# A two-layer decoder trunk: Norm's rows one product later in the convolution and the first MLP product, every second low part of the next operand behind the weights' low part

## The chip, the cores and the metric

The kernel runs on one core of one Trainium2 chip. The metric is the device time of one execution in microseconds (us), lower is better. TensorE (PE) has a queue of its own for weight loads (PEld); VectorE (DVE), ScalarE (ACT), GpSimd (POOL) and SyncE (SP, which issues most transfers) each work through their instructions in the order in which they were written down for that engine.

## The reference

Two residual layers over 1024 tokens of width 1024, all in fp32; layer 0 has an attention and pooling mixer, layer 1 a short gated convolution. Each layer then has cross-attention into 256 memory tokens and a squared-ReLU MLP of width 4096. Every sub-layer begins with an RMS norm.

```python
def rms_norm(x, g):
    xf = x.astype(jnp.float32)
    y = xf * lax.rsqrt(jnp.mean(xf * xf, axis=-1, keepdims=True) + EPS)
    return (y * g.astype(jnp.float32)).astype(x.dtype)
...
def odd_mixer(h, w_in, conv_w, w_out):
    S = h.shape[1]
    proj = h @ w_in
    b_gate = proj[..., :CONV_DIM]
    c_gate = proj[..., CONV_DIM:2 * CONV_DIM]
    z = c_gate * proj[..., 2 * CONV_DIM:]
    zp = jnp.pad(z, ((0, 0), (CONV_WIDTH - 1, 0), (0, 0)))
    y = zp[:, 0:S] * conv_w[0]
    for tap in range(1, CONV_WIDTH):
        y = y + zp[:, tap:tap + S] * conv_w[tap]
    return (b_gate * y) @ w_out
...
def sq_relu_mlp(h, w1, w2):
    a = jax.nn.relu(h @ w1)
    return (a * a) @ w2
...
    for l in range(DEPTH):
        ...
        h = h + cross_attention(rms_norm(h, norm_xattn_g[l]), mem_n,
                                xattn_wq[l], xattn_wkv[l], xattn_wo[l])
        h = h + sq_relu_mlp(rms_norm(h, norm_mlp_g[l]), mlp_w1[l], mlp_w2[l])
    return rms_norm(h, final_norm_g)
```

## The kernel before, in words

Activations lie transposed in SBUF: eight tiles of 128 channels x 1024 tokens. A matrix product keeps fp32 accuracy with three matmuls in place of one: operand and weight are each cut into a high part (a rounded copy, made by ACT: `h` tiles, `wh`) and a low part (the rest, made by DVE: `l` tiles, `wl`), and high x high, low x high and high x low are added up in PSUM. The cut is two instructions, L72 and L73:

```python
            nc.scalar.activation(hi, src, AF.Copy)
            nc.vector.tensor_sub(lo, src, f32(hi))
```

**Products.** The convolution's input projection, the query projection and both MLP matrices run as `split_steps`: a 2x2 block product in seven steps (i = 0 to 6) of 12 matmuls 128x512 each, with sums of operand blocks and of weight blocks in place of the eighth step. The operand has four groups of four tiles (`m0A0_g_j` is group g, tile j of chunk 0 of the MLP's hidden operand in layer 0; `m0x_g_j` is the convolution's operand, `c0o_x_g_j` that of layer 0's first MLP matrix). The weights are cut into four groups as well, `wh81_0`/`wl81_0` to `wh81_3`/`wl81_3` for weight pair 81; steps 0 and 1 use group 0, steps 2 and 3 group 1, and so on. `w_next()` runs at steps 0, 2, 4 and 6 and writes down the cut of a group one ahead of its use, so group 0 of the next product is cut at step 6. Of `wh` and `wl` there are two buffers each. A first-group cut also writes the sums of the weight halves (L162, L163, L165, L166: 128x512 on DVE). After a step `out(i)` moves a PSUM bank to SBUF (ACT copy or DVE add, at high priority).

**Hooks.** All other work (the next sub-layer's cuts, squares, taps, loads and stores) is hung on the steps as `hooks`: `{step: [functions]}`. At step i the weight cut is written down first, then the hooks, then the twelve matmuls and `out(i)`. A tile scheduler makes the final order of each engine from this, and each engine then keeps to it.

**Norm.** The row norms aren't applied to the operand; the product runs on the raw operand and its result is scaled by a row vector. `Norm.stage1` transposes the sum of squares on PE (eight 128x128 transposes, L354), reduces it on DVE (L355, L357) and takes the power -1/2 on POOL (L358, `rcol`). `Norm.stage2` spreads `rcol` over the partitions with eight PE transposes (L367) and copies them with ACT (L369, `rbc`).

**Layer stages by name.** `m0a`p / `m1a`p: product p (0 to 15) of the first MLP matrix in layer 0 / 1; `m0b`c`_`p: the second matrix, chunk c (0 to 3), product p (0 to 3); `cv`j`c`, `cv`j`x`, `cv`j`b`: the three projections of the convolution for channel pair j (0 to 3); products 0 and 1 of `ma`, and c and x of cv0, run in turns. `mlp.up` writes the first matrix's products, `prepare` the cuts of the next chunk's operand (`fetch` loads, `ready` cuts). The gate, the taps and the scaling of the convolution for pair j are hooks of its `b` product. The conv product's squares of `rbc` (`squared`) feed the gate.

Of the kernel before, what the change touches and what calls it, by code (L numbers as in the profile page):

```python
# [40 lines left out]
def hybrid_trunk(ctx: ExitStack, tc: tile.TileContext, xT, memT, vecs, lams, rel, onehot, negrow, invcnt,  # L41
# [284 lines left out]
    def merged(*hooks):  # L326
        return {i: [f for h in hooks for f in h.get(i, ())] for i in range(7)}
# [70 lines left out]
    X = Act()  # L398
# [513 lines left out]
    X, nrm = residual(Y, G_X[0], "X1", split=True)  # L912
# [140 lines left out]
    def mlp(l, X, nrm, g_next, name):  # L1053
# [46 lines left out]
        def fetch(c, g, js=range(KT // 2)):  # L1100
            def run():
                for j in js:
                    t = slot(f"{name}f{c}_{g}_{j}")
                    raw[c, g, j] = t if g < 3 else t[:, :H]
                    nc.sync.dma_start(raw[c, g, j], gd[4 * c + j][g])

            return run

        def ready(c, g, js=range(KT // 2)):
            def run():  # L1110
                for j in js:
                    A[c].group(g, j, raw.pop((c, g, j)))

            return run


        def prepare(c, left):
            if left == 3:
                return {1: [fetch(c, 0, (0, 1))], 4: [ready(c, 0, (0,))], 5: [ready(c, 0, (1,))]}
            if left == 2:  # L1120
                return {1: [fetch(c, 0, (2, 3))], 4: [ready(c, 0, (2,))], 5: [ready(c, 0, (3,))]}
            if left == 1:
                return {2: [fetch(c, 1)], 4: [fetch(c, 2)], 5: [ready(c, 1, (0,))], 6: [ready(c, 1, (1, 2)), fetch(c, 3)]}
            if left == 0 and c == 0:
                return {0: [ready(c, 1, (3,))], 2: [ready(c, 2, (1,))], 3: [ready(c, 2, (2,))], 4: [ready(c, 3, (2, 3))]}
            return {0: [ready(c, 1, (3,))], 1: [ready(c, 2, (0,))], 2: [ready(c, 2, (1, 2))],
                    3: [ready(c, 2, (3,))], 4: [ready(c, 3)]} if left == 0 else {}

        rest, ahead = merged(X.late, {5: [nrm.stage1], 6: [nrm.stage2]}), []
        r0, one = up(0, rest, False)  # L1130
        rest, two = up(1, {4: r0[1], 5: r0[2], 6: r0[3]}, False)
        in_turns(one, two)
        rest = merged(rest, {4: r0[5]})
        for p in range(2, 2 * KT):
            if p == 2 * KT - 1:
                ahead.extend(h_load(i, f"{name}b0") for i in range(2))
# [3 lines left out]
        rest = {}  # L1140
# [16 lines left out]
        def first_group(p):  # L1157
            nx.group(0, p, raws_x[p, 0])
# [6 lines left out]
        def get(g):  # L1165
            for p in range(2):
                x = slot(f"{name}xf{g}_{p}")
                raws_x[p, g] = x if g < 3 else x[:, :H]
                nc.sync.dma_start(raws_x[p, g], xd[p, g])

        def made(g, *ps):
            for p in ps:
                nx.group(g, p, raws_x.pop((p, g)))
        for c in range(4):
            for p in range(KT // 2):
                t, ahead = ahead, []
# [23 lines left out]
                if c == 0 and p < 2:  # L1200
                    todo.append(late[p])
                if tail and not fin:
                    todo.append({2: [lambda: get(1)], 4: [lambda: made(1, 0)],
                                 5: [lambda: scale(t, p, 0), lambda: first_group(p), lambda: made(1, 1)],
                                 6: [lambda: made(1, 2), lambda: get(2)]})
                elif tail:
                    todo.append({3: [squares_of(0, 0)], 5: [squares_of(1, 0)], 6: [squares_of(1, 1), lambda: nn.stage1((0,))]})
                steps = split_steps(A[c], f"{name}b{c}_{p}", evac, merged(*todo), tail=tail)
# [49 lines left out]
    def conv_mixer(X, nrm, g_next, name):  # L1258
        Y, ys = Halves(), {}
        sq = {}  # L1260

        def product(nm, hooks, first=False, run=True):
            r = [slot(f"{nm}_r{n}") for n in range(2)]

            def evac(n, h, ps, new):
                d = r[n][:, half(h)]
                if new:
                    nc.scalar.activation(d, ps, AF.Copy)
                else:
                    nc.vector.tensor_add(d, d, ps)  # L1270

            steps = split_steps(X, nm, evac, hooks, first=first)
            if not run:
                return r, steps
            for _ in steps:
                pass
            return r

        def parts(k):
            return lambda: Y.put(f"{name}g{k}_", k, ys.pop(k))  # L1280

        def squared():
            sq[0] = slot(f"{name}_rsq")
            nc.scalar.activation(sq[0], nrm.rbc, AF.Square)

        for j in range(KT // 2):
            nm, last = f"{name}{j}", j == KT // 2 - 1
            if j == 0:
                c, one = product(f"{nm}c", X.late[0], first=True, run=False)
                x, two = product(f"{nm}x", X.late[1], run=False)  # L1290
                in_turns(one, two)
            else:
                c = product(f"{nm}c", merged(before, {4: [parts(0)]} if last else {}))
                x = product(f"{nm}x", {1: [parts(1)], 3: [parts(2)]} if last else {})

            def gate(n, c=c, x=x):
                def run():
                    nc.vector.tensor_mul(c[n], c[n], x[n])
                    nc.vector.tensor_mul(c[n], c[n], sq[0])
                return run  # L1300

            def taps(n, z=c, j=j):
                def run():
                    k = 2 * j + n
                    y = ys[k] = slot(f"{name}_y{k}")
                    nc.scalar.activation(y, z[n], AF.Copy, scale=col(C_CONV + 16 + k))
                    for d in (1, 2):
                        nc.vector.scalar_tensor_tensor(y[:, d:], z[n][:, : S - d], col(C_CONV + 8 * (2 - d) + k),
                                                       y[:, d:], op0=ALU.mult, op1=ALU.add)
                return run  # L1310

            def scaled(n, j=j):
                return lambda: nc.vector.tensor_mul(ys[2 * j + n], ys[2 * j + n], nrm.rbc)

            hooks = {0: [gate(0)], 1: [taps(0)], 2: [gate(1)], 3: [taps(1)], 4: [scaled(0)], 5: [scaled(1)]}
            if j == 0:
                hooks = {1: [nrm.stage2, squared], 2: [gate(0)], 3: [taps(0)], 4: [gate(1)], 5: [taps(1)],
                         6: [scaled(0), scaled(1)]}
            if last:
                hooks = merged(hooks, {3: [parts(3)], 5: [parts(4)], 6: [parts(5)]})  # L1320
            b = product(f"{nm}b", hooks)

            def times(n, j=j, b=b):
                return lambda: nc.vector.tensor_mul(ys[2 * j + n], ys[2 * j + n], b[n])

            before = {1: [times(0)], 2: [times(1)]}
        for n in range(2):
            times(n)()
            parts(KT - 2 + n)()
        return residual(Y, g_next, f"{name}o", split=True, late=True)  # L1330
# [101 lines left out]
```

## Time and profile before

| what | value |
|---|---|
| median of three runs | 2512.99 us (2510.22 to 2517.41) |
| profiled execution | 2511.44 us, of which 2509.7 us from the first to the last instruction |
| mean granted TensorE clock | 0.997 |
| PE busy | 2466.0 us, 98% |
| DVE busy | 1842.6 us, 73% |
| ACT busy | 1133.6 us, 45% |
| POOL busy | 29.8 us, 1% |
| read from HBM, written | 252.53 MB, 116.65 MB |

PE is busy nearly all the time, so the span is PE's own work plus the few holes in it. A row of the timeline has the start in us, the length in us, the engine, the line, the operation, the tiles written and read, a count, and in brackets the idle time of the engine just before and what ended it. Tile numbers are left out in the trace: `wl` is any low part of weights, `m0A_3l` tile 3's low part of any group. A matmul row is 0.39 us long, though matmuls start closer together, since they are pipelined. The profile lists a wait only where the engine stood idle; a wait shorter than the overlap of two matmuls shows in the starts alone.

### The profile page before, as it was taken

How to read it: one execution, taken by the hardware profiler on the slowest of the kernel's cores; microseconds unless marked ns; L12 is line 12 of the kernel's file. 1: busy time of each engine (PE TensorE's matmuls, PEld its weight loads, DVE VectorE, ACT ScalarE, POOL GpSimd, SP SyncE). 2: the span in 40 equal slices, each digit the busy share in tenths (PEclk: the TensorE clock that was granted, in tenths of full speed). 3: DMA queues.
4: the chain of work that ended last, by engine and by line, in shares of the span. 5: the costliest groups of instructions: out<-in, count | busy, mean ns of one | idle time of the engine just before them, and what ended most of it. 6: DMA issues, size and time to landing. Idle time of an engine off the chain costs nothing.

```text
span 2509.7 us, 29710 instructions
## 1 busy us (share of the span) xinstructions
PE 2466.0 (98%) x11378; PEld 2021.3 (81%) x11378; DVE 1842.6 (73%) x2465; ACT 1133.6 (45%) x1610; POOL 29.8 (1%) x24
## 2 busy tenths in 40 slices
PE   9999999999999999999999999999999999999997
PEld 6777778888888887888887888888888888788886
DVE  7777764757577778987798777576677777888876
ACT  5455664436444334443355334454544343433432
POOL 0000000000000000000000000000000000000001
PEclk9999999999999999999999999999999999999998
DMA  5101256221324445787762121422233434777852
GB/s 178 34 26 51 68 163 204 103 89 55 126 85 150 160 163 202 275 302 253 268 222 84 52 63 55 168 68 84 76 109 123 168 142 160 290 271 246 285 201 92
DMA packets 110157, 371.11 MB, mean 148 GB/s; under 512 B 12608, under 2 KB 15040, under 8 KB 110016
## 3 DMA queue, kind: packets, MB, share of 16 engines
q1 hardware_dynamic: 75744, 255.44, 30.2%
q10 hardware_dynamic: 34272, 113.79, 11.8%
q8 instruction: 89, 1.46, 0.2%
q14 instruction: 52, 0.43, 0.1%
HBM read 252.53 MB, written 116.65 MB: 147 GB/s over the span
## 4 chain that ended last, share of the span: by engine, by line
PE 88%; DVE 7%; ACT 3%; issue 1%; DMA 1%; POOL 1%; SPq 0%; DVEq 0%; ACTq 0%; POOLq 0%
PE m0a_x L298 7%; PE m1a_x L298 7%; PE m0b_x L298 7%; PE m1b_x L298 6%; PE m0a_yz L298 5%; PE m1a_yz L298 5%; PE m0b_yz L298 5%; PE m1b_yz L298 5%; PE cvo L212 3%; PE X L212 3%; PE c0o L212 3%; PE c1o L212 3%; PE kv_ps L764 3%; PE qkv L212 2%; PE u L212 2%; PE c1q_x L298 2%
## 5 line engine op out<-in xcount | busy, mean ns | idle before, releaser
L72 ACT ACTIVATE wh<-wr 128x1024 fp32r<-128x1024 f32 (+1 forms) x330 | 313.0, 949 | 648.2 <-PE m1b_yz L298 132.0
L73 DVE TENSOR_TENSOR wl<-wr,wh 128x1024 fp32r<-128x1024 f32 (+1 forms) x330 | 358.4, 1086 | 163.7 <-ACT wh L72 159.8
L72 ACT ACTIVATE wh<-wt 128x1024 fp32r<-128x1024 f32 x84 | 88.8, 1057 | 85.9 <-PE m1b_x L298 14.4
L73 DVE TENSOR_TENSOR wl<-wt,wh 128x1024 fp32r<-128x1024 f32 x84 | 102.3, 1218 | 0.7 <-ACT wh L72 0.7
L212 PE MATMUL cvo<-cvg,wh 128*128 128x512 f32 x256 | 69.8, 389 | 0.0
L212 PE MATMUL X<-Y,wh 128*128 128x512 f32 x256 | 69.7, 389 | 0.0
L603 ACT ACTIVATE s_p<-s,s_negm 128x128 f32<-128x128 f32 (+7 forms) x64 | 47.3, 740 | 33.6 <-DVE s_negm L602 30.3
L162 DVE TENSOR_TENSOR wt<-wr 128x512 f32<-128x512 f32 x82 | 56.3, 686 | 6.8 <-DMA wr<-in_w_dram 3.1
L163 DVE TENSOR_TENSOR wt<-wr,wt 128x512 f32<-128x512 f32 x82 | 56.5, 688 | 1.5
L165 DVE TENSOR_TENSOR wr<-wr,wr 128x512 f32<-128x512 f32 x82 | 56.3, 686 | 1.0
L212 PEld LDWEIGHTS cvo<-cvg,wh 128*128 128x128 f32 x256 | 48.0, 188 | 10.4 <-ACT wh L72 0.4
L166 DVE TENSOR_TENSOR wr<-wr,wt 128x512 f32<-128x512 f32 x82 | 56.1, 684 | 0.0
L212 PEld LDWEIGHTS X<-Y,wh 128*128 128x128 f32 x256 | 48.0, 188 | 10.0
L1063 ACT ACTIVATE m0a_r<-m0a_r 128x1024 f32<-128x1024 f32 x32 | 34.0, 1061 | 30.0 <-DVE m0a_r L1062 29.9
L1063 ACT ACTIVATE m1a_r<-m1a_r 128x1024 f32<-128x1024 f32 x32 | 34.0, 1061 | 30.0 <-DVE m1a_r L1062 29.9
L602 DVE TENSOR_REDUCE s_negm<-s 128x1 f32<-128x128 f32 (+7 forms) x64 | 46.5, 749 | 0.2
L1073 ACT ACTIVATE m0a_r<-m0a_x 128x512 f32<-128x512 f32 x32 | 19.2, 599 | 55.6 <-PE m0a_x L298 55.6
L1073 ACT ACTIVATE m1a_r<-m1a_x 128x512 f32<-128x512 f32 x32 | 19.2, 599 | 55.4 <-PE m1a_x L298 52.0
L1077 DVE TENSOR_TENSOR m0a_r<-m0a_r,m0a_yz 128x512 f32<-128x512 f32 x32 | 21.9, 685 | 27.8 <-PE m0a_yz L298 27.6
L1077 DVE TENSOR_TENSOR m1a_r<-m1a_r,m1a_yz 128x512 f32<-128x512 f32 x32 | 21.9, 685 | 27.7 <-PE m1a_yz L298 27.4
L212 PE MATMUL X<-Y,wl 128*128 128x512 f32 x128 | 40.7, 389 | 0.0
L212 PE MATMUL cvo<-cvg,wl 128*128 128x512 f32 x128 | 40.6, 389 | 0.0
(2165 smaller groups left out, 7721.3 us busy)
## 6 DMA issues: line engine op xcount, KB each, us to landing
wr<-in_w_dram SPq DMA_DIRECT2D x128, 512.0 KB, 4.2
m0f<-m0a_d SPq DMA_DIRECT2D x48, 512.0 KB, 6.3
m1f<-m1a_d SPq DMA_DIRECT2D x48, 512.0 KB, 6.1
wr<-in_wkv_dram SPq DMA_DIRECT2D x32, 512.0 KB, 3.5
m0a_d<-m0a_r ACTq DMA_DIRECT2D x32, 512.0 KB, 3.0
m1a_d<-m1a_r ACTq DMA_DIRECT2D x32, 512.0 KB, 2.9
wr<-in_conv_in_dram SPq DMA_DIRECT2D x24, 512.0 KB, 3.5
wr<-in_wq_dram SPq DMA_DIRECT2D x16, 512.0 KB, 3.7
```

The source lines that it names most:

```text
L72: nc.scalar.activation(hi, src, AF.Copy)
L73: nc.vector.tensor_sub(lo, src, f32(hi))
L162: nc.vector.tensor_add(t[:, 4:], b[:, :4], b[:, 4:])
L163: nc.vector.tensor_sub(t[:, :4], a[:, :4], t[:, 4:])
L165: nc.vector.tensor_sub(a[:, :4], b[:, :4], a[:, :4])
L166: nc.vector.tensor_add(a[:, 4:], a[:, 4:], t[:, :4])
L212: nc.tensor.matmul(ps, wt[:, k, :], act.part(k, i, h), start=(k == 0 and wt is hi and i == 0), stop=(k == ks - 1 and wt is lo))
L298: nc.tensor.matmul(banks[b], w[a][:, 4 * (i % 2) + j, :], act.part(g, s, j, c), start=(new and j == 0 and n == 0), stop=(j == nk - 1 and n ...
L602: nc.vector.tensor_reduce(s["negm"][:, m : m + 1], ps[:, :L], axis=AX.X, op=ALU.max, negate=True)
L603: nc.scalar.activation(s["pr"][m][:, :L], ps[:, :L], AF.Exp, bias=s["negm"][:, m : m + 1], accum_out=s["den"][:, m : m + 1])
L764: nc.tensor.matmul(ps[mt], mem["x"][i][k // 4][:, k % 4, mt * P : (mt + 1) * P], w[j][:, kk, :], start=(k == 0 and n == 0), stop=(k == KT ...
L1063: nc.scalar.activation(t, t, AF.Square)
```

## The change

Nothing is added to or taken from the work: each engine has as many instructions as before. The hooks move.

- `prepare`: the cut of tiles 1 and 3 of the next chunk's group 0 moves from step 5 to step 6, where the next product's weight cut is written first.
- `up`: `Norm.stage2` and, with it, the squares, sums and stores of product 0 move one place later (stage2 from step 6 of product 0 to step 4 of product 1).
- the last product of layer 0's MLP (`tail`): cuts of the convolution's operand one step later.
- `conv_mixer`: `stage2` and `squared` one step later, gate and taps after them too; the scaling by `rbc` moves to the next product for pair 0, and one step later for the others.

```diff
         def prepare(c, left):
             if left == 3:
-                return {1: [fetch(c, 0, (0, 1))], 4: [ready(c, 0, (0,))], 5: [ready(c, 0, (1,))]}
+                return {1: [fetch(c, 0, (0, 1))], 4: [ready(c, 0, (0,))], 6: [ready(c, 0, (1,))]}
             if left == 2:
-                return {1: [fetch(c, 0, (2, 3))], 4: [ready(c, 0, (2,))], 5: [ready(c, 0, (3,))]}
+                return {1: [fetch(c, 0, (2, 3))], 4: [ready(c, 0, (2,))], 6: [ready(c, 0, (3,))]}
...
-        rest, ahead = merged(X.late, {5: [nrm.stage1], 6: [nrm.stage2]}), []
+        rest, ahead = merged(X.late, {5: [nrm.stage1]}), []
         r0, one = up(0, rest, False)
-        rest, two = up(1, {4: r0[1], 5: r0[2], 6: r0[3]}, False)
+        rest, two = up(1, {4: [nrm.stage2], 5: r0[1], 6: r0[2]}, False)
         in_turns(one, two)
-        rest = merged(rest, {4: r0[5]})
+        rest = merged({0: r0[3], 2: r0[5]}, rest)
...
                 if tail and not fin:
-                    todo.append({2: [lambda: get(1)], 4: [lambda: made(1, 0)],
-                                 5: [lambda: scale(t, p, 0), lambda: first_group(p), lambda: made(1, 1)],
-                                 6: [lambda: made(1, 2), lambda: get(2)]})
+                    todo.append({2: [lambda: get(1)], 5: [lambda: made(1, 0), lambda: scale(t, p, 0)],
+                                 6: [lambda: first_group(p), lambda: made(1, 1, 2), lambda: get(2)]})
...
-            hooks = {0: [gate(0)], 1: [taps(0)], 2: [gate(1)], 3: [taps(1)], 4: [scaled(0)], 5: [scaled(1)]}
+            hooks = {0: [gate(0)], 1: [taps(0)], 2: [gate(1)], 3: [taps(1)], 5: [scaled(0)], 6: [scaled(1)]}
             if j == 0:
-                hooks = {1: [nrm.stage2, squared], 2: [gate(0)], 3: [taps(0)], 4: [gate(1)], 5: [taps(1)],
-                         6: [scaled(0), scaled(1)]}
+                hooks = {2: [nrm.stage2, squared], 3: [gate(0)], 4: [taps(0)], 5: [gate(1)], 6: [taps(1)]}
...
             before = {1: [times(0)], 2: [times(1)]}
+            if j == 0:
+                before = merged({0: [scaled(0)], 1: [scaled(1)]}, before)
```

What the scheduler makes of it, at three places (the number behind a tile's last underscore is the scheduler's own count). First DVE at the end of `m0a14`, where the first low part of the weights of `m0a15` (`wl81_0`) is made. Before:

```order
L1062 SCALAR_TENSOR_TENSOR m0a14_r1_8138<-m0a14_r1_8138,c0o_rbc_6369 128x1024
L73 TENSOR_TENSOR m0A0_0_3l_8249<-m0f0_0_3_8162,m0A0_0_3h_8248 128x1024
L1075 COPY m0a14_r0_8137<-m0a14_x_8139 128x512
L73 TENSOR_TENSOR wl81_0_8266<-wr81_0_8069,wh81_0_8265 128x1024
L73 TENSOR_TENSOR wl81_1_8296<-wt81_8267,wh81_1_8295 128x1024
```

And of the change:

```order
L1062 SCALAR_TENSOR_TENSOR m0a14_r1_8138<-m0a14_r1_8138,c0o_rbc_6390 128x1024
L73 TENSOR_TENSOR wl81_0_8262<-wr81_0_8069,wh81_0_8261 128x1024
L1075 COPY m0a14_r0_8137<-m0a14_x_8139 128x512
L165 TENSOR_TENSOR wr81_0_8069<-wr81_1_8071,wr81_0_8069 128x512
L166 TENSOR_TENSOR wr81_0_8069<-wr81_0_8069,wt81_8263 128x512
L73 TENSOR_TENSOR m0A0_0_3l_8271<-m0f0_0_3_8162,m0A0_0_3h_8270 128x1024
L73 TENSOR_TENSOR wl81_1_8296<-wt81_8263,wh81_1_8295 128x1024
```

The low part of the next operand's tile 3 now stands behind `wl81_0`, and behind the copy and the two weight sums, ahead of `wl81_1`.

Second, PE in `cv0b`, the third product of the convolution, where the eight transposes L367 of `m0b_rcol` stand. Before:

```order
L298 MATMUL cv0b_x_11218<-m0x_0_3h_10849,wl100_0_11178 128x512
L298 MATMUL cv0b_yz_11219<-m0x_0_0h_10469,wh100_0_11177 128x512
L298 MATMUL cv0b_yz_11219<-m0x_0_0l_10470,wh100_0_11177 128x512
L298 MATMUL cv0b_yz_11219<-m0x_0_0h_10469,wl100_0_11178 128x512
L367 MATMUL m0b_b0_11238<-ident_69,m0b_rcol_8466 128x128 x4
L367 MATMUL m0b_b1_11244<-ident_69,m0b_rcol_8466 128x128 x4
L298 MATMUL cv0b_yz_11219<-m0x_0_1h_10622,wh100_0_11177 128x512
L298 MATMUL cv0b_yz_11219<-m0x_0_1l_10623,wh100_0_11177 128x512
L298 MATMUL cv0b_yz_11219<-m0x_0_1h_10622,wl100_0_11178 128x512
```

And of the change:

```order
L298 MATMUL cv0b_yz_11219<-m0x_0_2h_10793,wh100_0_11177 128x512
L298 MATMUL cv0b_yz_11219<-m0x_0_2l_10794,wh100_0_11177 128x512
L298 MATMUL cv0b_yz_11219<-m0x_0_2h_10793,wl100_0_11178 128x512
L298 MATMUL cv0b_yz_11219<-m0x_0_3h_10872,wh100_0_11177 128x512
L298 MATMUL cv0b_yz_11219<-m0x_0_3l_10873,wh100_0_11177 128x512
L298 MATMUL cv0b_yz_11219<-m0x_0_3h_10872,wl100_0_11178 128x512
L367 MATMUL m0b_b0_11255<-ident_69,m0b_rcol_8466 128x128 x4
L367 MATMUL m0b_b1_11261<-ident_69,m0b_rcol_8466 128x128 x4
L298 MATMUL cv0b_x_11218<-m0x_1_0h_10842,wh100_1_11220 128x512
L298 MATMUL cv0b_x_11218<-m0x_1_0l_10843,wh100_1_11220 128x512
```

The transposes now stand behind all 24 matmuls of steps 0 and 1, nine matmuls later, where the second weight group (`wh100_1`) begins. In `m0a0` and `m1a0` the transposes of `c0o_rcol` and `c1o_rcol` likewise move behind the twelve matmuls of step 6.

Third, DVE and then ACT at the start of `cv0c`, where its first weight group (`wl98_0`) and the second (`wh98_1`) are cut. DVE before:

```order
L1189 TENSOR_TENSOR m0b3h6_10695<-m0b3h6_10695,m0b3_3_yz_10735 128x512
L73 TENSOR_TENSOR m0x_1_1l_10854<-m0xf1_1_10778,m0x_1_1h_10853 128x1024
L1189 TENSOR_TENSOR m0b3h6_10695<-m0b3h6_10695,m0b3_3_x_10734 128x512
L73 TENSOR_TENSOR wl98_0_10872<-wr98_0_10665,wh98_0_10871 128x1024
L73 TENSOR_TENSOR m0x_1_2l_10881<-m0x2_t0_10797,m0x_1_2h_10880 128x1024
L165 TENSOR_TENSOR wr98_0_10665<-wr98_1_10667,wr98_0_10665 128x512
```

DVE of the change:

```order
L1189 TENSOR_TENSOR m0b3h6_10695<-m0b3h6_10695,m0b3_3_yz_10735 128x512
L73 TENSOR_TENSOR wl98_0_10864<-wr98_0_10665,wh98_0_10863 128x1024
L1189 TENSOR_TENSOR m0b3h6_10695<-m0b3h6_10695,m0b3_3_x_10734 128x512
L165 TENSOR_TENSOR wr98_0_10665<-wr98_1_10667,wr98_0_10665 128x512
L166 TENSOR_TENSOR wr98_0_10665<-wr98_0_10665,wt98_10865 128x512
L73 TENSOR_TENSOR m0x_1_1l_10877<-m0xf1_1_10778,m0x_1_1h_10876 128x1024
L73 TENSOR_TENSOR wl99_0_10921<-wr99_0_10820,wh99_0_10920 128x1024
L73 TENSOR_TENSOR m0x_1_2l_10881<-m0x2_t0_10797,m0x_1_2h_10880 128x1024
L73 TENSOR_TENSOR wl98_1_10958<-wt98_10865,wh98_1_10957 128x1024
```

ACT before:

```order
L72 ACTIVATE m0x_1_2h_10880<-m0x2_t0_10797 128x1024
L72 ACTIVATE wh99_0_10920<-wr99_0_10820 128x1024
L844 DMA m0b3hd6_11144<-m0b3h6_10695 128x1024
L1149 ACTIVATE m0x3_r1_10901<-m0b3h6_10695,vec_76 128x512
L1149 ACTIVATE m0x3_r1_10901<-m0b3h7_10697,vec_76 128x512
L72 ACTIVATE wh98_1_10957<-wt98_10873 128x1024
```

ACT of the change:

```order
L72 ACTIVATE wh99_0_10920<-wr99_0_10820 128x1024
L844 DMA m0b3hd6_11144<-m0b3h6_10695 128x1024
L72 ACTIVATE m0x_1_2h_10880<-m0x2_t0_10797 128x1024
L72 ACTIVATE wh98_1_10957<-wt98_10865 128x1024
L1149 ACTIVATE m0x3_r1_10901<-m0b3h6_10695,vec_76 128x512
L1149 ACTIVATE m0x3_r1_10901<-m0b3h7_10697,vec_76 128x512
```

On DVE the low parts of the operand's tiles 1 and 2 of group 1 moved behind `wl98_0`; on ACT the cut `wh98_1` moved ahead of the two scalings L1149 that the sums behind them (`m0x3_t0`, `m0x_1_3`) read.

## Rows read from the trace of the kernel before

**Rows 1.** the page: busy time by engine; the chain that ended last.

```profile
PE 2466.0 (98%) x11378; PEld 2021.3 (81%) x11378; DVE 1842.6 (73%) x2465; ACT 1133.6 (45%) x1610; POOL 29.8 (1%) x24
...
PE 88%; DVE 7%; ACT 3%; issue 1%; DMA 1%; POOL 1%; SPq 0%; DVEq 0%; ACTq 0%; POOLq 0%
```

**Rows 2.** PE's waits, longest in total first: us in total, times, longest.

```profile
PE m0b_b L367 <- POOL m0b_rcol L358: 3.6, 1, 3.6
...
PE cv0c_x L298 <- DVE wl L73: 1.6, 1, 1.6
...
PE c0o_b L367 <- POOL c0o_rcol L358: 1.4, 1, 1.4
...
PE m0a_x L298 <- DVE wl L73: 1.3, 1, 1.3
...
PE m1b_x L298 <- DVE wl L73: 0.5, 2, 0.3
...
PE m0b_x L298 <- DVE wl L73: 0.4, 1, 0.4
```

**Rows 3.** windows: length, busy us (count) of PE, PEld, DVE, ACT, POOL; clock; DMA.

```profile
1018.00:1050.00 32.00, 31.63 (x139) 25.27 (x138) 30.48 (x37) 18.84 (x22) 0.00 (x0) 1.00 0.60 235
1100.00:1140.00 40.00, 40.00 (x177) 32.97 (x177) 35.60 (x46) 17.91 (x21) 0.00 (x0) 1.00 0.73 261
1376.00:1380.00 4.00, 3.63 (x14) 3.26 (x15) 0.00 (x0) 2.19 (x3) 0.32 (x1) 0.58 0.00 0
```

**Rows 4.** timeline, `m0a0` and its stage 2.

```profile
738.17 2.06 POOL L358 TENSOR_TENSOR c0o_rcol<-c0o_ms,mhalf 128x8 f32<-128x8 f32 x1 [218.81 <-DVE c0o_ms L357]
...
738.52 0.39 PE L298 MATMUL m0a_yz<-c0o_x_3h,wl 128*128 128x512 f32 x1
...
740.29 1.09 PE L367 MATMUL c0o_b<-ident,c0o_rcol 128*128 128x128 f32 x8 [1.38 <-POOL c0o_rcol L358]
...
741.13 0.71 PE L298 MATMUL m0a_x<-c0o_x,wh 128*128 128x512 f32 x2
```

**Rows 5.** timeline, start of `m0a15`.

```profile
1000.17 1.22 DVE L73 TENSOR_TENSOR m0A_3l<-m0f,m0A_3h 128x1024 fp32r<-128x1024 f32 x1
...
1001.50 0.39 PE L298 MATMUL m0a_yz<-c0o_x_0l,wh 128*128 128x512 f32 x1
1001.90 1.21 DVE L73 TENSOR_TENSOR wl<-wr,wh 128x1024 fp32r<-128x1024 f32 x1
...
1003.17 0.50 PE L298 MATMUL m0a_x<-c0o_x_0h,wl 128*128 128x512 f32 x1 [1.28 <-DVE wl L73]
```

**Rows 6.** timeline, start of `cv0c`.

```profile
1327.64 1.22 DVE L73 TENSOR_TENSOR m0x_1l<-m0xf,m0x_1h 128x1024 fp32r<-128x1024 f32 x1
...
1328.65 0.39 PE L298 MATMUL cv0c_yz<-m0x_0l,wh 128*128 128x512 f32 x1
...
1329.38 1.21 DVE L73 TENSOR_TENSOR wl<-wr,wh 128x1024 fp32r<-128x1024 f32 x1
...
1330.64 0.50 PE L298 MATMUL cv0c_x<-m0x_0h,wl 128*128 128x512 f32 x1 [1.61 <-DVE wl L73]
```

**Rows 7.** timeline, `cv0b` and its stage 2.

```profile
1371.87 2.35 DVE L1298 TENSOR_TENSOR cv0c_r<-cv0c_r,cv0x_r 128x1024 f32<-128x1024 f32 x2
...
1372.04 4.28 POOL L358 TENSOR_TENSOR m0b_rcol<-m0b_ms,mhalf 128x8 f32<-128x8 f32 x1 [631.80 <-DVE m0b_ms L357]
...
1372.35 0.39 PE L298 MATMUL cv0b_yz<-m0x_0h,wl 128*128 128x512 f32 x1
1374.14 0.68 DVE L162 TENSOR_TENSOR wt<-wr 128x512 f32<-128x512 f32 x1
...
1376.37 1.97 PE L367 MATMUL m0b_b<-ident,m0b_rcol 128*128 128x128 f32 x8 [3.63 <-POOL m0b_rcol L358]
...
1379.64 0.39 PE L298 MATMUL cv0b_yz<-m0x_2l,wh 128*128 128x512 f32 x1
```

**Rows 8.** source line L358, POOL: count, shortest/median/longest ns, first and last start.

```profile
L358 POOL TENSOR_TENSOR sub_rcol<-sub_ms,mhalf x4: 1636/1640/2547, 134.1 to 353.9; 128x8 f32<-128x8 f32 x4
```

## The prediction

> **What bounds the kernel now.** I read the page first. PE is busy 98% of the span and is 88% of the chain that ended last, with DVE 7%, ACT 3% and POOL 1% [rows 1]: a faster kernel is one in which PE's holes shrink, since no matmul is taken out. So the second view is the list of PE's waits [rows 2]: what I look for there are the holes at the places that the change touches. Six kinds are: the transposes of stage 2 in the convolution (3.6 us behind POOL), the same in the first MLP product of each layer (1.4 each; layer 1 has the same row for `c1o_b`), and low parts of weights that DVE makes too late (`cv0c` 1.6, `m0a` 1.3, and `m1a` with a row of the same size, and 0.4 and 0.5 in the second MLP product of the two layers). Third come the timeline rows around each, since a wait costs more or less than its idle time: matmuls overlap. In an undisturbed stretch 177 matmuls fill 40.00 us [rows 3], so 0.226 us from start to start; I count a loss as the distance of two starts, less the work that belongs between them.
>
> **Stage 2 in the first MLP product.** The last matmul before the transposes starts at 738.52, the first behind them at 741.13 [rows 4]: 2.61 us, of which 0.23 is the first one's own and 0.84 (740.29 to 741.13) the eight transposes. Lost: 1.54. Cause: POOL's power ran 738.17 to 740.23. After the change twelve matmuls of step 6, 12 x 0.226 = 2.71 us, stand between; PE reaches the transposes at 738.52 + 0.23 + 2.71 = 741.46, which is 1.2 after `rcol`. The wait goes, in both layers: 2 x 1.54 = 3.1. The squares, sums and stores that wait for `rbc` come later too; who needs them is the load of the next chunk's operand many products on, so I put them at nothing. Bound: if POOL were held there as long as in the convolution (4.28 us, below), `rcol` came at 742.45 and 1.0 of the 1.54 stayed.
>
> **The low part of the next operand at `m0a15`.** PE's start jumps from 1001.50 to 1003.17 because `wl81_0` starts only at 1001.90, and ahead of it DVE made `m0A0_0_3l` from 1000.17 [rows 5]. Lost: 1.67 - 0.23 = 1.44, and 0.11 more in the first matmul after it (0.50 long in place of 0.39). After the change `wl81_0` takes the place at 1000.17 and ends at 1001.4; PE wants it at 1001.50 + 0.23 = 1001.73. The wait goes: 1.55, in both layers 3.1. What is late next is `wl81_1`, now behind the copy, two weight sums and the moved low part: 1001.4 + 3 x 0.6 + 1.14 = 1004.3, its own end 1005.5; PE, four of the product's 24 matmuls on that group done by 1001.73, asks for it 22 starts later, at 1001.73 + 22 x 0.226 = 1006.7. Slack 1.2. This edit is made at 16 places in all (tiles 1 and 3, four chunks, two layers). The other fifteen I put at nothing where DVE has idle time (35.60 busy of 40.00 in the second product's middle [rows 3]): the moved instruction only changes places in a queue that has holes. At the start of the second MLP product DVE is busy 30.48 of 32.00 while PE has the small waits of 0.4 and 0.5 [rows 3, 2]; there the work put back is asked for within the same stretch, so I take half of 0.9, 0.45, with ends at -1 and +0.9.
>
> **The start of the convolution.** PE's start jumps from 1328.65 to 1330.64 for `wl98_0`, which DVE began at 1329.38, behind the low part `m0x_1_1l` at 1327.64 and an add [rows 6]. Lost: 1.99 - 0.23 + 0.11 = 1.87. With `wl98_0` at 1327.64 it ends at 1328.85, and PE wants it at 1328.88: gone, by a hair. But the order gives something back. ACT's cut `wh98_1` has to wait until PE has let go of `wh98_0`, 20 matmuls after 1328.88, so at 1333.4, and now stands ahead of the two scalings that stood ahead of it before. An estimate from the lengths in rows 5 and 6 and the order: the cut ends at 1334.5, the two scalings (0.67 each) at 1335.8; then DVE has four sums and adds of 128x512 (0.60 from start to start), a low part (1.13), four more of 128x512, a low part, two sums, and `wl99_1` itself (1.21): 10 x 0.60 + 2 x 1.13 + 1.21 = 9.5, so 1345.3. PE asks for `wl99_1` when 70 more matmuls are done (the rest of 72 of `cv0c` and `cv0x`, and two), at 1328.88 + 15.8 = 1344.7. A new wait of 0.6, with what hangs on it 0.75. Gain 1.87 - 0.75 = 1.1; ends 0 (all of it comes back) and 1.87.
>
> **Stage 2 in the convolution.** From the start at 1372.35 to that at 1379.64 there are 7.29 us, which hold five matmuls (1.13) and eight transposes (0.84 at full clock): 5.32 lost [rows 7, 4]. More than the 3.6 of the list, for after the wait the granted clock was 0.58 in 1376 to 1380, the lower of the two levels for part of it, 1.2 in place of 2.4 GHz [rows 3]; transposes and the next four matmuls ran at that. Now the transposes have nine more matmuls ahead: PE reaches them at 1372.35 + 10 x 0.226 = 1374.61. If POOL's power took what it takes elsewhere (1.64 [rows 8], 2.06 [rows 4]), `rcol` would be there at 1374.1 and nothing would be left. But here it took 4.28 [rows 7]. It began at 1372.04, when DVE had just started two gate multiplications (1371.87, 2.35 us), and then came L162 from 1374.14 to 1374.82, all of them with both inputs in SBUF and back to back; 1374.82 + 1.64 = 1376.46, close to the 1376.32 at which `rcol` came. I read it as POOL held until DVE left a hole. The change's DVE order there is the same up to L162, so `rcol` comes at 1376.32 again and PE waits 1376.37 - 1374.61 = 1.76, and 0.11. I expect full clock behind it: the waits of 1.61 and 1.28 are followed by a matmul of 0.50 at once [rows 6, 5], while here 3.63 was needed for the fall. Gain 5.32 - 1.87 = 3.45. Ends: 0 (POOL held longer, clock falls again) and 5.32.
>
> The Trainium skill, page "SBUF — State Buffer", section "Who interferes with whom", says that a DVE instruction with two SBUF inputs contends with a GpSimd instruction that reads SBUF, and that whoever issues second blocks fully. By that rule the wait keeps its 1.76 us and the sum is the one I take; without it the sum would be 1.9 us better. The trace's 4.28 against 1.64 agrees.
>
> Behind the transposes DVE's chain of gate, taps and scalings now starts little earlier while PE is 3.5 earlier, so `wl101_0`, the first low part of `cv1c`, gets close: I count it ready some 0.5 before it is wanted. Moving the scalings out of `cv0b` is what keeps that room. Nothing taken.
>
> **Sum.** 3.1 + 3.1 + 0.45 + 1.1 + 3.45 = 11.2 us. Against the profiled execution's own 2511.44 that is 2500.2. The median of the runs lies 1.55 above that execution, inside their spread of 7.2, so I stay near: 2500.5.
>
> **Rivals.**
>
> (1) All touched waits go and nothing comes back: 3.1 + 3.1 + 0.9 + 1.87 + 5.32 = 14.3, so 2497. For it: the list shows each wait with one cause, and each cause moves. Against: POOL's 4.28 has its cause on DVE, which stays, and the start of the convolution is full on both DVE and ACT.
>
> (2) The waits move more than they go. The 1.87 of `cv0c` comes back whole, the second MLP product loses 1, and in the convolution POOL is held until after the next DVE work, so that wait and low clock stay: 3.1 + 3.1 - 1 = 5.2, so 2506. For it: DVE is the second engine of the chain and near full at both places. Against: in `cv0b` DVE runs out of work after L162, until PE has done step 1.
>
> (3) Slower. The moved low part pushes `wl_1` of the next product over its slack at all 16 places. At `m0a15` it has 1.2 us; beyond that each place would cost a wait like the one of rows 5, 1.55: 16 x 1.55 = 24.8, less the other gains (11.2 - 3.1 = 8.1), so 17 slower, 2528. It decides at 1.2 us of DVE work more than I count ahead of `wl_1`. Against: the stretch of rows 3 has 4.4 us of DVE idle time in 40.
>
> (4) The change does next to nothing: if the waits were bound by data that come from elsewhere (a load, an ACT cut). Against: each row names DVE or POOL, and the DVE queue ahead of each is back to back; 2511.
>
> **How the numbers follow.** 0.3% is about what a measurement of this kernel can tell from no change, 7.5 us: the border is at 2505.5. Forecast (2498 to 2504): 0.50. Rival 1 (2494 to 2498, since waits too short for the list may go with the others): 0.22. Rival 2 (2504 to 2509): 0.20, of which a third still counts as faster. Rival 3: 0.04. Rival 4: 0.04. Faster: 0.50 + 0.22 + 0.07 = 0.79; slower 0.04; the same 0.17. The range 2494 to 2507 leaves out the upper part of rival 2, and rivals 3 and 4.
>
> **What would show it.** Right: no wait of `c0o_b` and `c1o_b` in the list, none of `m0a_x` and `m1a_x`; `m0b_b` still there at 1.5 to 1.8 with clock 1.00 behind it; POOL's L358 in `cv0b` again some 4.3 long; `cv0c_x` gone, and a smaller new wait for a low part some 14 us later. Wrong: L358 at 2 us (then rival 1), `m0b_b` above 2.5 with a lower clock (rival 2), or new rows of `m0b_x` and `m0a_x` behind DVE in many products (rival 3).

## The result and the profile after

The changed kernel took 2499.52 us (median of six runs, 2498.28 to 2503.3) against 2512.03 (2510.22 to 2517.41): a ratio of 0.9945, 95% interval 0.9935 to 0.9955, or 12.5 us faster. The page of its profiled execution (2502.05 us), first lines:

```profile
span 2500.1 us, 29716 instructions
...
PE 2464.3 (99%) x11378; PEld 2022.4 (81%) x11378; DVE 1842.4 (74%) x2465; ACT 1133.9 (45%) x1610; POOL 30.1 (1%) x24
```

PE's busy time is 1.7 us less than before and the span 9.6: most of what went is idle time of PE. The list of PE's waits, the rows at the changed places (us in total, times, longest), which answer to [rows 2]:

```profile
PE m0b_b L367 <- POOL m0b_rcol L358: 1.6, 1, 1.6
...
PE cv0c_yz L298 <- DVE cv0c_r L1269: 0.8, 1, 0.8
...
PE m1b_x L298 <- DVE m1b0h L1189: 0.3, 1, 0.3
PE m0b_x L298 <- DVE m0b0h L1189: 0.3, 1, 0.3
```

The rows of `c0o_b`, `c1o_b`, `m0a_x`, `m1a_x` and `cv0c_x` are gone, `m0b_b` fell from 3.6 to 1.6, and `cv0c_yz` is new. Both kernels have 11378 PE instructions, in the same order but for the moved transposes and for matmuls of one size that the scheduler put in another order at some of the changed places (up to 60 in a row). So the start of PE's n-th instruction in one trace less that in the other shows where time was won. Steps of that difference, each read where it has settled again, layer 0 and layer 1, beside the terms of the prediction:

| place | predicted | layer 0 | layer 1 |
|---|---|---|---|
| stage 2 in the first MLP product | -1.54 each | -1.59, and -0.30 two products on | -1.63, and -0.25 |
| `wl81_0` at `m0a15` and its like in `m1a15` | -1.55 each | -1.53 | -1.51 |
| second MLP product | -0.45 in all | -0.95 +0.81 -0.41 -0.09 | -0.95 +0.84 -0.39 |
| second MLP product, waits behind a late load | 0 | -0.21 | -0.48 |
| start of the convolution | -1.87 +0.75 | -1.73 +1.14 | |
| stage 2 in the convolution | -3.45 | -3.43 | |
| start of the convolution's output product | 0 | -0.31 | |
| query projection of layer 1 | 0 | | +0.26 |
| sum | -11.2 | -12.7 | |

Two rows aren't a steady gain or loss of the change. The -0.21 and -0.48 stand in every other trace against that of before, the three in which `prepare` is as before among them. There the trace of before has waits that follow a load that landed late. The second, in layer 1 (ACT's cut of tile 3, its low part, the weights' low part, PE's matmul):

```profile
2297.16 1.06 ACT L72 ACTIVATE m1A_3h<-m1f 128x1024 fp32r<-128x1024 f32 x1 [1.66 <-DMA m1f<-m1a_d]
...
2298.26 1.23 DVE L73 TENSOR_TENSOR m1A_3l<-m1f,m1A_3h 128x1024 fp32r<-128x1024 f32 x1 [1.20 <-ACT m1A_3h L72]
...
2300.00 1.22 DVE L73 TENSOR_TENSOR wl<-wr,wh 128x1024 fp32r<-128x1024 f32 x1
...
2301.27 0.50 PE L298 MATMUL m1b_x<-m1A_0h,wl 128*128 128x512 f32 x1 [0.19 <-DVE wl L73]
```

The low part that waits for the load stands ahead of `wl`, and PE waits for both. With the new `prepare` it stands behind `wl`, and none of the six traces that have it shows such a wait; of the four without it, the trace of before does. (A third wait of PE for `wl`, at 1137 us, stands in all four and costs 0.09 to 0.45 by the starts; the -0.09 is its share here.) The +0.26 in the query projection is no part of the change either: the four later variants of the changed kernel, measured below, have -0.03 or -0.04 there. Without these two rows the change is worth 12.3 us by the starts.

The spans differ by 9.6 only, since this execution lost 3.0 us at another place, which the change doesn't touch and which the last section takes up, and 0.1 in small steps ahead of the first changed place.

The timeline of the changed kernel around stage 2 in `m0a0` answers to [rows 4] (start, length, engine, line, operation, tiles, count); POOL, the eight transposes, and the matmul behind them:

```profile
741.33 2.07 POOL L358 TENSOR_TENSOR c0o_rcol<-c0o_ms,mhalf 128x8 f32<-128x8 f32 x1 [218.81 <-DVE c0o_ms L357]
...
744.57 1.03 PE L367 MATMUL c0o_b<-ident,c0o_rcol 128*128 128x128 f32 x8
...
745.36 0.48 PE L298 MATMUL m0a_x<-c0o_x_0h,wh 128*128 128x512 f32 x1
```

`rcol` is there at 743.40 and PE comes at 744.57: the transposes take 0.79 and nothing waits. Around `m0a15`, against [rows 5]:

```profile
1001.50 1.22 DVE L73 TENSOR_TENSOR wl<-wr,wh 128x1024 fp32r<-128x1024 f32 x1
...
1002.60 0.39 PE L298 MATMUL m0a_yz<-c0o_x_0h,wh 128*128 128x512 f32 x1
...
1002.83 0.44 PE L298 MATMUL m0a_x<-c0o_x_0h,wl 128*128 128x512 f32 x1
...
1005.57 1.22 DVE L73 TENSOR_TENSOR wl<-wt,wh 128x1024 fp32r<-128x1024 f32 x1
...
1008.12 0.39 PE L298 MATMUL m0a_x<-c0o_x_0h,wl 128*128 128x512 f32 x1
```

The first `wl` is `wl81_0`: from 1001.50, and PE goes from 1002.60 to 1002.83, its next start. The low part `m0A0_0_3l` follows at 1004.43, `wl81_1` at 1005.57, ready at 1006.79, and PE reads it in the third matmul of its step, at 1008.12: 1.33 of slack, where I had 1.2. Around the start of `cv0c`, against [rows 6]:

```profile
1326.57 1.22 DVE L73 TENSOR_TENSOR wl<-wr,wh 128x1024 fp32r<-128x1024 f32 x1
...
1327.84 0.50 PE L298 MATMUL cv0c_x<-m0x_0h,wl 128*128 128x512 f32 x1
...
1332.54 1.06 ACT L72 ACTIVATE wh<-wt 128x1024 fp32r<-128x1024 f32 x1 [2.68 <-PE cv0c_yz L298]
...
1333.50 1.32 ACT L1149 ACTIVATE m0x_r<-m0b3h,vec 128x512 f32<-128x512 f32 x2
1333.63 1.23 DVE L73 TENSOR_TENSOR wl<-wt,wh 128x1024 fp32r<-128x1024 f32 x1 [0.64 <-ACT wh L72]
...
1339.12 0.68 DVE L1269 TENSOR_TENSOR cv0c_r<-cv0c_r,cv0c_yz 128x512 f32<-128x512 f32 x1
...
1339.86 0.50 PE L298 MATMUL cv0c_yz<-m0x_0h,wh 128*128 128x512 f32 x1 [0.77 <-DVE cv0c_r L1269]
```

`wl98_0` (1326.57) now comes in time but for a few hundredths: PE's matmul starts at 1327.84 and is 0.50 long. Then ACT cuts `wh98_1` at 1332.54, the scalings L1149 follow, DVE stands idle 0.64 for that cut, and its first add from `cv0c`'s banks (L1269) comes so late that PE waits 0.77 for it at 1339.86. Around stage 2 in `cv0b`, against [rows 7], and the windows behind it:

```profile
1370.37 4.28 POOL L358 TENSOR_TENSOR m0b_rcol<-m0b_ms,mhalf 128x8 f32<-128x8 f32 x1 [626.98 <-DVE m0b_ms L357]
...
1372.47 0.68 DVE L162 TENSOR_TENSOR wt<-wr 128x512 f32<-128x512 f32 x1
...
1372.70 0.39 PE L298 MATMUL cv0b_yz<-m0x_3h,wl 128*128 128x512 f32 x1
...
1374.71 1.09 PE L367 MATMUL m0b_b<-ident,m0b_rcol 128*128 128x128 f32 x8 [1.62 <-POOL m0b_rcol L358]
...
1375.55 0.48 PE L298 MATMUL cv0b_x<-m0x_0h,wh 128*128 128x512 f32 x1
```

```profile
300.00:308.00 8.00, 8.00 (x26) 5.87 (x27) 4.09 (x8) 1.93 (x5) 0.00 (x0) 0.57 0.21 66
1374.00:1378.00 4.00, 3.29 (x19) 2.87 (x20) 2.22 (x3) 2.16 (x4) 0.65 (x1) 1.00 0.40 120
```

POOL's power took 4.28 again. It ended at 1374.65, and PE went from 1372.70 to 1374.71, 2.01 in place of 0.23; the clock behind it was 1.00 (1374 to 1378), the transposes took 0.84 up to the next matmul at 1375.55.

### The profile page after: what moved, and what is told of

It reads as the page before. It is cut to its first block, busy times and chain, and to the rows that moved or that the text cites. A ratio compares the mean times of both kernels' runs of the same rounds, so it can differ in the third digit from the quotient of the medians.

```text
span 2500.1 us, 29716 instructions
## 1 busy us (share of the span) xinstructions
PE 2464.3 (99%) x11378; PEld 2022.4 (81%) x11378; DVE 1842.4 (74%) x2465; ACT 1133.9 (45%) x1610; POOL 30.1 (1%) x24
## 4 chain that ended last, share of the span: by engine, by line
PE 90%; DVE 5%; ACT 3%; issue 1%; POOL 0%; DMA 0%; SPq 0%; DVEq 0%; ACTq 0%; POOLq 0%
PE m0a_x L298 7%; PE m1a_x L298 7%; PE m1b_x L298 7%; PE m0b_x L298 7%; PE m1a_yz L298 5%; PE m0a_yz L298 5%; PE m1b_yz L298 5%; PE m0b_yz L298 5%; PE cvo L212 3%; PE X L212 3%; PE c0o L212 3%; PE c1o L212 3%; PE kv_ps L764 3%; PE qkv L212 2%; PE u L212 2%; PE c1q_x L298 2%
## 5 line engine op out<-in xcount | busy, mean ns | idle before, releaser
L162 DVE TENSOR_TENSOR wt<-wr 128x512 f32<-128x512 f32 x82 | 56.2, 686 | 6.9 <-DMA wr<-in_wq_dram 3.1
L163 DVE TENSOR_TENSOR wt<-wr,wt 128x512 f32<-128x512 f32 x82 | 56.4, 687 | 1.3
```

The lines of the kernel that those rows point to most:

```text
L162: nc.vector.tensor_add(t[:, 4:], b[:, :4], b[:, 4:])
L163: nc.vector.tensor_sub(t[:, :4], a[:, :4], t[:, 4:])
```

## The experiments

**One part at a time.** Each of the four edits alone, on the kernel before.

The cuts of `prepare` alone:

```diff
-                return {1: [fetch(c, 0, (0, 1))], 4: [ready(c, 0, (0,))], 5: [ready(c, 0, (1,))]}
+                return {1: [fetch(c, 0, (0, 1))], 4: [ready(c, 0, (0,))], 6: [ready(c, 0, (1,))]}
...
-                return {1: [fetch(c, 0, (2, 3))], 4: [ready(c, 0, (2,))], 5: [ready(c, 0, (3,))]}
+                return {1: [fetch(c, 0, (2, 3))], 4: [ready(c, 0, (2,))], 6: [ready(c, 0, (3,))]}
```

> The kernel before with the move in prepare alone (cut of tiles 1 and 3 at step 6 in place of 5). Theory that the gain is a sum of separate waits: the row of m0a_x and m1a_x behind wl is gone (1.45 each in the starts), the small waits at the start of the second MLP product go and come back later (0.94 saved, 0.6 to 0.7 given back per layer, some 0.7 more in the products after it): 4.5 to 5 us faster, ratio 0.998. Rival, that the moves only work together since DVE is one queue: under 2 us here. Rival, that the low parts behind cost elsewhere: slower than before.

Measured: ratio 0.9967 (0.9954 to 0.9979). PE's starts moved by -1.53 and -1.49 at `m0a15` and `m1a15`, by -0.95 and then +0.85 at the start of the second MLP product of layer 0 (-0.95 and +0.87 in layer 1), and by -0.73 and -0.88 in its later products: 4.8 in all, of which 0.21 and 0.48 are the waits behind a late load. Its list of PE's waits:

```profile
PE m0b_b L367 <- POOL m0b_rcol L358: 3.6, 1, 3.6
...
PE cv0c_x L298 <- DVE wl L73: 1.6, 1, 1.6
...
PE c0o_b L367 <- POOL c0o_rcol L358: 1.3, 1, 1.3
...
PE m0b_x L298 <- DVE m0b0h L1189: 0.3, 1, 0.3
```

The waits of the other three edits stand as before, those of `m0a_x` and `m1a_x` are gone, and `m0b_x` now waits for an add of DVE (L1189) in place of a low part: that is the time given back.

Stage 2 of the first MLP product alone:

```diff
-        rest, ahead = merged(X.late, {5: [nrm.stage1], 6: [nrm.stage2]}), []
+        rest, ahead = merged(X.late, {5: [nrm.stage1]}), []
...
-        rest, two = up(1, {4: r0[1], 5: r0[2], 6: r0[3]}, False)
+        rest, two = up(1, {4: [nrm.stage2], 5: r0[1], 6: r0[2]}, False)
...
-        rest = merged(rest, {4: r0[5]})
+        rest = merged({0: r0[3], 2: r0[5]}, rest)
```

> The kernel before with the move of stage 2 in the first MLP product alone. Separate waits: c0o_b and c1o_b leave the list of waits, 1.7 at the transposes and 0.25 in the product after it, in both layers: 3.9 us faster, ratio 0.9984. Rival of moves that only work together: under 1.5 us. Rival that PE meets the later squares or stores: another wait in m0a1 or m0a2, gain under 2.

Measured: ratio 0.9979 (0.9971 to 0.9988). `c0o_b` and `c1o_b` have no row; the others stay:

```profile
PE m0b_b L367 <- POOL m0b_rcol L358: 3.6, 1, 3.6
...
PE cv0c_x L298 <- DVE wl L73: 1.6, 1, 1.6
...
PE m0a_x L298 <- DVE wl L73: 1.3, 1, 1.3
```

PE's starts moved by -1.89 in layer 0 and -1.88 in layer 1. In the profiled execution the unchanged stage 2 of the convolution cost 1.1 more than in the trace of before, with the same wait of 3.6: its granted clock was 0.50 from 1374 to 1380, where the trace of before has 0.50 and 0.65 in the two windows 1376 to 1380.

The tail of layer 0's MLP alone:

```diff
-                    todo.append({2: [lambda: get(1)], 4: [lambda: made(1, 0)],
-                                 5: [lambda: scale(t, p, 0), lambda: first_group(p), lambda: made(1, 1)],
-                                 6: [lambda: made(1, 2), lambda: get(2)]})
+                    todo.append({2: [lambda: get(1)], 5: [lambda: made(1, 0), lambda: scale(t, p, 0)],
+                                 6: [lambda: first_group(p), lambda: made(1, 1, 2), lambda: get(2)]})
```

> The kernel before with the move in the tail of layer 0's MLP alone. Separate waits: cv0c_x behind wl (1.75 in the starts) goes, and a new wait of 1.1 comes some 12 us later, on DVE's add of the first bank of cv0c (L1269), because the two scalings stand behind wh98_1 on ACT: 0.6 us faster, not to be told from no change in the times, but both in the rows. Rival, that the new wait comes from another part of the change: it isn't in this trace and the gain is 1.75.

Measured: ratio 0.9992 (0.9984 to 1.0001), not to be told from no change. In the starts -1.71 and +1.17; the new wait is in the list, the old one of `cv0c_x` isn't:

```profile
PE cv0c_yz L298 <- DVE cv0c_r L1269: 0.8, 1, 0.8
```

So the new wait is this edit's own.

The convolution alone (the last two hunks of the change):

```diff
-                hooks = {1: [nrm.stage2, squared], 2: [gate(0)], 3: [taps(0)], 4: [gate(1)], 5: [taps(1)],
-                         6: [scaled(0), scaled(1)]}
+                hooks = {2: [nrm.stage2, squared], 3: [gate(0)], 4: [taps(0)], 5: [gate(1)], 6: [taps(1)]}
...
+            if j == 0:
+                before = merged({0: [scaled(0)], 1: [scaled(1)]}, before)
```

> The kernel before with the moves in the convolution alone. Separate waits: m0b_b falls from 3.6 to 1.6 with full clock behind it, POOL's power (L358) again 4.28 long: 3.5 us faster, ratio 0.9986. Rival, that the wait fell because the work before it came earlier by the other parts: m0b_b stays near 3.6 or POOL's power is another length.

Measured: ratio 0.9977 (0.9968 to 0.9986). -3.47 at stage 2 and -0.31 at the start of the convolution's output product, L358 4.28 long; two rows of its list:

```profile
PE cv0c_x L298 <- DVE wl L73: 1.6, 1, 1.6
PE m0b_b L367 <- POOL m0b_rcol L358: 1.6, 1, 1.6
```

The four gains by PE's starts at their own places, 4.8, 3.8, 0.5 and 3.8, make 12.9, against 12.7 together; without the late loads and the query projection it is 12.2 against 12.3. The waits are separate. By the ratios (0.33, 0.21, 0.08 and 0.23%) they make 0.85%, against 0.55% (0.45 to 0.65): each has an interval of about 0.1% to both sides, and they share one set of runs of the kernel before, with a median of 2513.95, where the changed kernel was held against 2512.03 (the last section shows what lies between the two). For gains of this size the starts are the better measure.

**POOL held by DVE.** The changed kernel, the gate's factors in the other order, so that no gate multiplication can run before `rbc` is there:

```diff
-                    nc.vector.tensor_mul(c[n], c[n], x[n])
-                    nc.vector.tensor_mul(c[n], c[n], sq[0])
+                    for f in (sq[0], x[n]) if j == 0 else (x[n], sq[0]):
+                        nc.vector.tensor_mul(c[n], c[n], f)
```

> The changed kernel, with the two factors of the gate of channel pair 0 in the other order (first the square of rbc, then the x product; the same result up to rounding), so that no multiplication of the gate can stand on DVE while POOL makes rcol. Theory that POOL is held by back-to-back DVE instructions with two SBUF inputs: POOL's power (L358) for m0b_rcol falls from 4.28 to 2.0 to 2.6, rcol is there before PE has done step 1, m0b_b leaves the list of waits (1.6, 1.75 in the starts), and the kernel is 1.7 us faster than the changed one unless the four multiplications behind rbc make a low part of cv1c late. Rival, that POOL is long there for a reason of its own (its place after a long idle time, or DMA): 4.28 stays and so does m0b_b.

Measured: 2497.56 us (2496.8 to 2502.27), ratio to before 0.9944 (0.9930 to 0.9957). Timeline around the power:

```profile
1371.48 0.69 DVE L162 TENSOR_TENSOR wt<-wr 128x512 f32<-128x512 f32 x1
...
1371.60 2.06 POOL L358 TENSOR_TENSOR m0b_rcol<-m0b_ms,mhalf 128x8 f32<-128x8 f32 x1 [627.12 <-DVE m0b_ms L357]
...
1372.20 0.69 DVE L163 TENSOR_TENSOR wt<-wr,wt 128x512 f32<-128x512 f32 x1
...
1373.97 0.39 PE L298 MATMUL cv0b_yz<-m0x_3h,wl 128*128 128x512 f32 x1
...
1374.20 1.03 PE L367 MATMUL m0b_b<-ident,m0b_rcol 128*128 128x128 f32 x8
```

L358 took 2.06 and PE ran on from 1373.97 to 1374.20; -1.82 in the starts against the changed kernel, and no new wait in `cv1c`, although four multiplications now stand behind `rbc`.

The changed kernel with one more multiplication of DVE (its result is read by nothing):

```diff
                     nc.vector.tensor_mul(c[n], c[n], x[n])
+                    if (j, n) == (0, 0):
+                        nc.vector.tensor_mul(x[n], x[n], x[n])
                     nc.vector.tensor_mul(c[n], c[n], sq[0])
```

> The changed kernel with one more DVE multiplication of 128x1024, both inputs in SBUF, between the gate's two and the evacuation, in the place of L162 (128x512), which comes later; nothing reads its result. POOL held by DVE: L358 for m0b_rcol grows by 1.13 - 0.60 = 0.53 to 4.8, and m0b_b from 1.6 to 2.15. Rival, a length of POOL's own: 4.28 and 1.6.

One run, 2499.13 us. The timeline of DVE and POOL, and the row of the wait:

```profile
1366.89 2.35 DVE L1297 TENSOR_TENSOR cv0c_r<-cv0c_r,cv0x_r 128x1024 f32<-128x1024 f32 x2
...
1367.06 4.81 POOL L358 TENSOR_TENSOR m0b_rcol<-m0b_ms,mhalf 128x8 f32<-128x8 f32 x1 [627.03 <-DVE m0b_ms L357]
...
1369.16 1.21 DVE L1299 TENSOR_TENSOR cv0x_r<-cv0x_r 128x1024 f32<-128x1024 f32 x1
...
1370.29 0.68 DVE L1269 TENSOR_TENSOR cv0b_r<-cv0b_r,cv0b_yz 128x512 f32<-128x512 f32 x1
```

```profile
PE m0b_b L367 <- POOL m0b_rcol L358: 2.1, 1, 2.1
```

4.81 and 2.1, +0.51 in the starts: longer by what DVE's back-to-back work is longer. A length of POOL's own is out.

**The new wait at the start of the convolution.** The changed kernel with another tail:

```diff
-                    todo.append({2: [lambda: get(1)], 5: [lambda: made(1, 0), lambda: scale(t, p, 0)],
-                                 6: [lambda: first_group(p), lambda: made(1, 1, 2), lambda: get(2)]})
+                    todo.append({2: [lambda: get(1)], 4: [lambda: made(1, 0)],
+                                 5: [lambda: scale(t, p, 0), lambda: made(1, 1)],
+                                 6: [lambda: first_group(p), lambda: made(1, 2), lambda: get(2)]})
```

> The changed kernel with another tail of layer 0's MLP: cut of tile 1 back at step 5, cut of the first group's last tile at step 6, so that on ACT the two scalings L1149 stand ahead of wh98_1 again, as before, and wl98_0 still stands ahead of a low part on DVE. Theory that the new wait of cv0c comes from that order on ACT: no wait of cv0c_x or cv0c_yz over 0.3, some 1.0 us faster than the changed kernel. Rival, that the wait comes from DVE's amount of work ahead of the add, whatever ACT's order: the wait stays within 0.3 of its 0.8.

Measured: 2497.47 us (2497.11 to 2502.17), ratio 0.9944 (0.9932 to 0.9957); -1.27 in the starts against the changed kernel, and no row of `cv0c` in the list. The timeline, DVE's `wl98_0`, the scalings, `wh98_1`, `wl98_1` and the add:

```profile
1322.24 1.22 DVE L73 TENSOR_TENSOR wl<-wr,wh 128x1024 fp32r<-128x1024 f32 x1
...
1325.60 1.34 ACT L1149 ACTIVATE m0x_r<-m0b3h,vec 128x512 f32<-128x512 f32 x2 [1.00 <-DVE m0b3h L1189]
...
1329.03 1.06 ACT L72 ACTIVATE wh<-wt 128x1024 fp32r<-128x1024 f32 x1 [2.10 <-PE cv0c_yz L298]
...
1331.19 1.22 DVE L73 TENSOR_TENSOR wl<-wt,wh 128x1024 fp32r<-128x1024 f32 x1
...
1334.06 0.68 DVE L1270 TENSOR_TENSOR cv0c_r<-cv0c_r,cv0c_yz 128x512 f32<-128x512 f32 x1
```

From `wl98_0` to the add there are 11.82 in place of 12.55 (1326.57 to 1339.12): most of what is missing is DVE's idle time of 0.64 for `wh98_1`, which the sums behind the two scalings now fill. But the edit also took `m0x_0_3l` from ahead of `wl98_0`, which starts 1.32 ahead of PE's first matmul of `cv0c` in place of 0.33. Both help; how much of the 1.14 each would undo alone wasn't separated. As an estimate from these rows, the order on ACT would take 0.73 off the 1.14 and the earlier `wl98_0` 0.99, so neither alone would end the wait. The rival, that DVE's work ahead of the add makes the wait whatever ACT's order, is weakened by this run and not ruled out.

**Both together.**

> The changed kernel with the other order of the gate's factors and the other tail together. If both waits are separate: 2.5 to 2.8 us faster than the changed kernel, some 15 faster than the one before, ratio 0.994.

Measured: 2495.68 us (2495.13 to 2495.74), ratio to before 0.9932 (0.9919 to 0.9944): 3.8 us under the changed kernel's median. The starts, which leave out the fall of the clock described below, say 3.0 (1.27 and 1.82, less 0.1 between the two places). Neither `m0b_b` nor `cv0c` is in its list; this is the fastest version tried.

## Why the prediction was right, and where its steps were off

**Stage 2 in the convolution** (3.45 forecast, 3.43 measured) went as worked out: POOL's end at the old distance from DVE's L162, a wait of 1.6 in the list, full clock behind it. That DVE's two-input instructions hold POOL, which the prediction read from one pair of rows, was then shown by taking them away (2.06) and by adding one (4.81). In all of these traces L358 ends 1.49 or 1.50 behind the end of the last instruction of the run: L162 in the traces of before and of the change and with the other order of factors, the added multiplication in the fourth. One word of the reading was too strong: POOL doesn't need a hole. In the run with one more multiplication, DVE's add from PSUM follows at 1370.29 without idle time, and POOL gets in. Where there is a hole, it can be tiny: with the other order of factors L163, with two SBUF inputs as well, starts 0.03 behind the end of L162, and POOL isn't held by it. The Trainium skill, page "SBUF — State Buffer", section "Who interferes with whom", says that a DVE instruction with at most one SBUF input doesn't contend with GpSimd outside the two-port modes; the add from PSUM agrees.

The prediction took more from that section than its words give. A rule that the second to issue blocks sets one instruction against one. Held by the first gate multiplication alone, which ended at 1373.08 in the trace of before, POOL would have ended 1.50 later, at 1374.58 (an estimate), and PE, there at 1374.61, would not have waited. That POOL stays held through a run of such instructions is what these traces show, 4.28 and 4.81.

**Stage 2 in the first MLP product** was right in its mechanism, its term too small: 1.59 and 1.63 for 1.54. I took the 0.84 from the first transpose to the next matmul as the price of eight transposes, but that row stands right behind the wait and has some of its cost in it; undisturbed they take 0.79 (744.57 to 745.36). And 0.30 and 0.25 more went two products on, where a low part had been a tenth late.

**`m0a15`** was right: 1.53 and 1.51 in the joint trace, 1.53 and 1.49 alone, for 1.55, and slack 1.33 at `wl81_1` for 1.2. The rival in which the moved low parts push 16 others over their slack didn't come about at a single place.

**The second MLP product** was mis-sized: 0.45 forecast, 1.14 measured (-0.64 and -0.50), or 1.83 with the waits behind late loads. I took half of the two listed waits, and read both as standing at the start of the product; of the 0.5 of `m1b_x` [rows 2], 0.19 is the wait at 2301.27 shown above, 110 us later. In the starts the first product's waits were 0.95 each, and of those most came back some 20 us later, as forecast, on DVE's add L1189:

```profile
1048.18 0.68 DVE L1189 TENSOR_TENSOR m0b0h<-m0b0h,m0b_x 128x512 f32<-128x512 f32 x1
...
1049.01 0.70 PE L298 MATMUL m0b_x<-m0A,wh 128*128 128x512 f32 x2 [0.27 <-DVE m0b0h L1189]
```

But the products behind had waits too that the list doesn't show, since they are shorter than the overlap of two matmuls, and these went for good (0.41 and 0.39 by the starts, in every trace with the new `prepare`).

**The start of the convolution**: the wait went (1.73 for 1.87) and a new one came (1.14 for 0.75), behind the ACT cut that I had named, and by the estimate above in part for its order; but not on `wl99_1`. It came some 4 us earlier (12.0 behind PE's first matmul on `wl98_0` in place of 15.8), on the add of the same DVE queue that stands ahead of it: PE's next matmul on `cv0c_yz` waits for it. I had asked of the queue's last instruction when it was due, and not of those ahead of it.

The 0.31 at the start of the convolution's output product was not in the forecast at all; it belongs to the moves in the convolution, whose trace alone has it too. The errors had both signs (-0.7 in each of the two MLP products, -0.3 in the output product, +0.5 at the start of the convolution), and the sum of 11.2 stood against 12.3 by the starts and 12.5 by the medians. So the largest terms were right by their mechanism; that the sum is off by 1.1 only is in part luck: had the start of the convolution come out as forecast, it would be off by 1.6.

## What to carry to other kernels

Where the busiest engine is at 98%, cost each short wait by the distance of two starts on both sides of it, and go through the starts of the whole stage: waits shorter than the pipeline's overlap are in no list, and here they were 1.7 of 12.3 us. Before a small gain is credited to an edit, look at the same place in traces that don't have the edit: here 0.7 us hung on when a load landed. When work is put behind a late instruction, ask of every instruction behind the new place when it is due, evacuations first. Before a small GpSimd instruction on the path, keep VectorE free of long runs with two SBUF inputs: the other order of two factors was worth 1.8 us.

## What the runs showed of the hardware that had not been expected

The clock can fall at a wait in one execution and not in the next of the same program. The same stretch, unchanged attention work, in the trace of before (length; PE, PEld, DVE, ACT, POOL busy with counts; clock; DMA):

```profile
300.00:308.00 8.00, 8.00 (x42) 6.23 (x42) 3.91 (x9) 4.92 (x9) 0.00 (x0) 1.00 0.19 66
```

In the changed kernel's profiled execution the same window has a granted clock of 0.57 (its row is shown above), so much of it at 1.2 in place of 2.4 GHz, and 26 matmuls and transposes in place of 42. The wait of PE ahead of it, for ACT at some 297 us, is 0.87 there and 0.88 in the trace of before. The fall cost 3.0 us by the starts. The profiled execution with the other order of the gate's factors had it as well (0.50, 4.4 us), the other eight had not. What decides it stays open; the length of the wait alone does not. The prediction took it that a wait of 3.63 was needed for a fall, and the four traces with a wait of 3.6 in the convolution do all show one behind it, those with 1.5 to 2.1 there none; but here a fall follows a wait of 0.87, and in other traces none follows 0.88.

The times of the kernel before fit this: of the 27 executions that the four parts were held against, 13 have a mean granted clock of 0.995 and took 2514.63 to 2517.41 us, and 14 have 0.996 or 0.997 and took 2510.68 to 2513.95 (where in them the clock was lower is not on record). A median over both lies where the mixture puts it, and 3 us are nearly the gain of one of the edits, which is why the parts were compared by the starts and not by the medians alone.
